# Writing a bias table to memory once, end first, instead of 129 times

## The chip, the core and the metric

The kernel runs on one core of one Trainium2 chip. A core has five engines that run side by side and wait for one another by semaphores: TensorE (PE, matrix products), VectorE (DVE), ScalarE (ACT), GpSimd (POOL) and SyncE (SP). 16 DMA engines move data between the device memory and the core's on-chip memory. The kernel starts its DMAs from three queues: SyncE's (q1 in the profile), ScalarE's (q10) and GpSimd's (q0). The metric is the device time of one execution in microseconds (us).

## The reference, cut to what matters

The program is three transformer blocks in a row over 256 tokens of width 1024. The change concerns only the first mixer, an attention with a selection of keys and a learned bias by the distance of key and query:

```
def t5_bucket(rel):            # 32 buckets of the distance key - query
    ...

def dsa_attention(q, k, v, iq, ik, iw, rel_bias):
    top_k = min(TOPK_MAX, seq // 4)                      # 64
    def block(i):
        s = einsum('bqhd,bsd->bqhs', iq_b, ik32) * idx_scale
        score = einsum('bqhs,bqh->bqs', relu(s), iw_b * w_scale)
        score = where(allowed, score, -inf)
        _, sel = lax.top_k(score, top_k)
        bias = rel_bias[t5_bucket(sel - t[None, :, None])]
        logits = einsum('bqhd,bqkhd->bhqk', q_b, k_sel) * att_scale + transpose(bias)
        p = softmax(where(valid, logits, -inf))
        return einsum('bhqk,bqkhd->bqhd', p, v_sel)
```

For each of 8 heads the bias depends on key minus query alone, so 384 numbers a head (distances -255 to 128) hold all that a block of 128 queries needs. Query row p wants a run of 256 of them whose start moves by one from row to row.

## The kernel before

The work goes through three mixers and two feed-forward blocks, then 16 experts. All weights are float32 and are split into a rounded part (`wh`, a cast on ScalarE, line 176) and a remainder (`wl`, a subtraction on VectorE or GpSimd, line 177) before TensorE uses them. This is done in *units* of 128x1024 numbers; a block of weights of 1 MB holds two units. Loads of blocks go out from SyncE into 5 buffers (`rawp`, line 67), so a load waits until the units of the block five loads before it are split. `take` (line 203) splits units three ahead of the one that TensorE is to use; there are 4 buffers each for `wh` and `wl`.

In the first mixer SyncE, ScalarE and GpSimd execute in the order in which the program issues; VectorE's and TensorE's order is fixed at build time. `ORDER_A` (line 1980) is the order of the program's steps. Those named below are:

- `iq0` to `iq7`, `aq0` to `aq3`, `ak0`, ...: one unit each of the projections, 24 matmuls of 256 columns (lines 237 to 239). Two units share a PSUM bank. For `iq`, each bank is emptied by two casts on ScalarE (line 740) and two subtractions on VectorE (line 741); only two banks exist (`psM`), so `iq6` cannot start before the bank of `iq2` and `iq3` is empty.
- `scb0` to `scb3`, `sca0`, `sca1`: selection scores (lines 747 to 766): matmuls, a Relu on ScalarE (757), multiply-adds on VectorE (763).
- `parms`: GpSimd issues 16 small loads of parameters (line 90). The last one, `gT`, is used by a multiplication on VectorE (`rw`, line 579) that stands in VectorE's order in front of the scores of `scb1`.
- `bias`: SyncE loads the bias rows (line 671) into `bias`, in the trace `b<-scr`.
- `selb0` to `selb7`, `sela0` to `sela7`: 8 rounds each of picking the 8 largest scores (lines 772, 773). In the last round the bias is added to the mask (line 779), half of the heads on VectorE and half on GpSimd: 128x1024 numbers each for the later 128 queries (`b<-b,score`), 128x512 for the first 128 (`ws<-b,score`).
- `lgb`, `lga`: logits, which take these sums (line 803).

The bias table comes about early: a one-hot matrix from `constants` (line 49) times `rel_bias` gives 8 rows of 384 numbers, ScalarE copies them from PSUM (line 664), and its queue then writes them to a scratch tensor in device memory 129 times for each head (lines 665, 666): 8 x 129 x 384 x 4 bytes = 1.585 MB. The load in line 671 steps by 383 numbers from one partition to the next, so that row p begins p numbers earlier in copy p of the table; that is what the copies are for.

Of the kernel before, what the change touches and what calls it, by code (L numbers as in the profile page):

```python
# [8 lines left out]
F32 = mybir.dt.float32  # L9
# [9 lines left out]
S = 256  # L19
# [9 lines left out]
def constants():  # L29

    p = np.arange(128)[:, None]
    f = np.arange(128)[None, :]
    eye = (p == f).astype(np.float32)
    upper = (p <= f).astype(np.float32)
    lower = (p >= f).astype(np.float32)
    base = np.concatenate([eye, upper, lower], axis=1).astype(np.float32)
    lev = []
    for b in (2, 4, 8, 16, 32, 64, 128):
        m = (p // b == f // b) & (p % b < b // 2) & (f % b >= b // 2)
        lev.append(m)  # L40
    lev = lev + [m.T for m in lev] + [p == f]
    levels = np.concatenate(lev, axis=1).astype(np.float32)
    rel = np.arange(384) - 255
    n = np.abs(rel)
    big = np.full(n.shape, 7)
    for edge in (8, 12, 16, 23, 32, 46, 64, 91):
        big = big + (n >= edge)
    bucket = np.where(rel > 0, 16, 0) + np.where(n < 8, n, big)
    onehot = (np.arange(32)[:, None] == bucket[None, :]).astype(np.float32)
    t = np.arange(S)  # L50
    inv = []
    for w in (2, 4, 8, 16):
        cnt = np.minimum(t + w - w // 2, S) - np.maximum(t - w // 2, 0)
        inv.append((np.float32(1.0) / cnt.astype(np.float32))[[*range(8), *range(S - 8, S)]])
    rows = np.concatenate([np.concatenate(inv), (t % 64 != 0).astype(np.float32), np.arange(CAP) + 1.0]).astype(np.float32)[None, :]
    return {"c_base": base, "c_levels": levels, "c_onehot": onehot, "c_rows": rows}


class Kernel:
# [569 lines left out]
    def mixer_ab(self):  # L629
        nc, I, sm = self.nc, self.I, self.sm  # L630
        with ExitStack() as st:
# [6 lines left out]
            onehot = sp.tile([32, 384], F32, name="onehot")  # L638
# [16 lines left out]
            p = self.mm()  # L655
# [6 lines left out]
            wsT = sp.tile([128, 8, 128], F32, name="wsT")  # L662
            bs = wsT[:8].rearrange("p a b -> p (a b)")[:, :384]
            nc.scalar.copy(bs, bt[:8, :384])
            scr = self.dram.tile([8, 129, 384], F32, name="scr")
            nc.scalar.dma_start(scr, bs[:, None, :].to_broadcast([8, 129, 384]))
            bias = b8()
            sc = scr[:, :, :]

            def bias_rows():  # L670
                self.load(bias, bass.AP(tensor=sc.tensor, offset=sc.offset + 127, ap=[[383, 128], [129 * 384, 8], [1, S]]))

            self.in_order("SP", "Activation", "Pool")
            kiw = sp.tile([80, S], F32, name="kiw")
# [70 lines left out]
            bp = {}  # L745

            def scores(t, h0, per):
# [17 lines left out]
                if h0 + 2 * per == 16:  # L765
                    nc.vector.memset(score[t][0:64, W - 64:W], NEG)

            def select(t, rounds):
                W = 128 * (t + 1)
                for i in rounds:  # L770
                    m8 = sm.tile([128, 8], F32, name="m8")
                    nc.vector.max(m8, score[t])
                    nc.vector.match_replace(score[t], m8, score[t], GONE)
                if rounds[-1] == 7:
                    nc.vector.tensor_scalar(score[t], score[t], GONE, NEG, op0=OP.not_equal, op1=OP.mult)
                    bp[t] = b8() if t else sp.tile([128, 8, 128], F32, name="ws")
                    for q in range(2):
                        a = slice(4 * q, 4 * q + 4)
                        self.on(f"bp{'ab'[t]}{q}").tensor_tensor(bp[t][:, a, :], bias[:, a, S - W:],
                                                                 score[t][:, None, :].to_broadcast([128, 4, W]), op=OP.add)  # L780

            qT = sp.tile([128, 4, S], F32, name="qT")
# [104 lines left out]
            def gated():  # L887
                for g in range(8):
# [5 lines left out]
            held, turns = [], []  # L894
            out = self.out_steps({0: ya, 4: yb}, ((0, 0), (1, 0), (0, 4), (1, 4)))
            steps = {"bias": bias_rows, "key0": index_keys, "key1": index_keys_turned, "parms": lambda: turns.extend(self.params(sp)),
                     "gvd": lambda: gv_done(held[0]), "gud": lambda: gu_done(held[1]), "gated": gated, "gate": gate,
                     "again": lambda: setattr(self, "g", self.gains())}
# [9 lines left out]
            for t, a in enumerate("ab"):  # L908
                steps.update((f"sel{a}{i}", lambda t=t, i=i: select(t, (i,))) for i in range(8))
                for q in range(2):  # L910
                    steps[f"ex{a}{q}"] = lambda t=t, q=q: expo(t, range(4 * q, 4 * q + 4))
                    steps[f"sh{a}{q}"] = lambda t=t, q=q: share(t, q)
                    steps[f"tu{a}{q}"] = lambda t=t, q=q: turn(t, q)
# [1171 lines left out]
```

## Time and profile before

| What | Before |
|---|---|
| median of 3 runs | 1848.58 us (1847.56 to 1848.87) |
| the profiled execution | 1848.39 us |
| its span in the trace | 1846.6 us |
| PE, DVE, ACT, POOL busy | 80%, 37%, 28%, 17% of the span |
| moved by q1, q10, q0 | 534.54, 1.59, 1.75 MB |

The page also cuts the span into 40 slices of 46 us and shows the busy share of each in tenths:

```profile
PE   7779999998899999889997566666566565656675
DVE  3675877758877777697410000000000000000001
...
DMA  8533654644335557322999999999999999999998
```

In the first three slices TensorE is less busy than in those after them. From slice 20 on the DMA engines are busy nearly all the time: the experts' weights. Between the two lies a long stretch in which TensorE is busy for 90% or more of most slices. [...]

### The profile page before, as it was taken

What the parts mean: (1) busy time and instruction counts of PE and PEld (TensorE: products, weight loads), DVE (VectorE), ACT (ScalarE), POOL (GpSimd) and SP (SyncE); (2) the same over time, 40 slices, a digit from 0 to 9 for tenths busy, and PEclk for the clock granted to TensorE, in tenths of its full rate; (3) what the DMA queues carried; (4) which work ended last, traced back from release to release, by engine and by line L of the source; (5) the groups of instructions that cost most, each with busy time, mean ns of one, the idle gap of its engine ahead of it and who ended that gap; (6) DMA issues with size and microseconds to landing.
All of it is one profiled execution on the core that took longest, in us unless ns stands there. A gap on an engine that the chain in (4) does not pass through costs nothing.

```text
span 1846.6 us, 22659 instructions
## 1 busy us (share of the span) xinstructions
PE 1468.6 (80%) x9340; PEld 923.8 (50%) x9340; DVE 692.1 (37%) x1143; ACT 518.0 (28%) x902; POOL 321.8 (17%) x339
## 2 busy tenths in 40 slices
PE   7779999998899999889997566666566565656675
PEld 6767999987779999778741111111111111111111
DVE  3675877758877777697410000000000000000001
ACT  4445655564446555553310000000000000000001
POOL 5453120044640001674200000000000000000000
PEclk9889999999999999899998778778877778887878
DMA  8533654644335557322999999999999999999998
GB/s 236 173 136 114 208 191 167 224 128 138 114 99 182 179 167 232 119 87 82 383 382 424 425 425 426 423 426 426 424 426 425 425 424 424 425 425 425 424 426 293
DMA packets 140665, 539.32 MB, mean 292 GB/s; under 512 B 6871, under 2 KB 85033, under 8 KB 109330
## 3 DMA queue, kind: packets, MB, share of 16 engines
q1 hardware_dynamic: 138434, 534.54, 73.8%
q10 hardware_dynamic: 1040, 1.59, 0.7%
q0 software_dynamic: 1088, 1.75, 0.4%
q8 instruction: 73, 1.20, 0.3%
q14 instruction: 30, 0.25, 0.0%
HBM read 535.21 MB, written 2.63 MB: 291 GB/s over the span
## 4 chain that ended last, share of the span: by engine, by line
DMA 47%; PE 37%; DVE 7%; issue 1%; ACT 1%; POOL 1%; POOLq 0%; DVEq 0%; SPq 0%; ACTq 0%
DMA w<-in_expert_w_up_dram 25%; DMA w<-in_expert_w_gate_dram 12%; DMA w<-in_expert_w_down_dram 10%; PE mm L237 3%; PE mm L238 3%; PE mm L239 3%; PE tp L237 2%; PE tp L238 2%; PE tp L239 2%; PE acc L956 2%; PE acc L958 2%; PE acc L957 2%; PE acc L249 2%; PE acc L250 2%; PE acc L251 2%
## 5 line engine op out<-in xcount | busy, mean ns | idle before, releaser
L1876 PE MATMUL mm<-w 128*32 128x512 f32 x1536 | 252.1, 752 | 157.7 <-DMA w<-in_expert_w_up_dram 101.6
L177 DVE TENSOR_TENSOR wl<-w,wh 128x1024 fp32r<-128x1024 f32 x180 | 248.1, 1381 | 66.0 <-ACT wh L176 65.5
L176 ACT CAST wh<-w 128x1024 fp32r<-128x1024 f32 x238 | 247.2, 1044 | 82.1 <-PE acc L958 35.9
L1896 PE MATMUL mm<-w,gain 128*32 128x512 f32 x512 | 165.8, 793 | 95.0 <-DMA w<-in_expert_w_down_dram 84.7
L1876 PEld LDWEIGHTS mm<-w 128*32 128x32 f32 x1536 | 50.7, 126 | 351.5 <-DMA w<-in_expert_w_up_dram 151.9
L1888 DVE TENSOR_TENSOR gain<-gain,mm 128x512 f32<-128x512 f32 x16 | 11.0, 688 | 561.3 <-PE mm L1876 561.3
L237 PE MATMUL mm<-xTh,wh 128*128 128x256 f32 x712 | 207.1, 291 | 12.6 <-DVE b L741 5.8
L238 PE MATMUL mm<-xTl,wh 128*128 128x256 f32 x712 | 205.3, 288 | 0.0
L239 PE MATMUL mm<-xTh,wl 128*128 128x256 f32 x712 | 205.0, 288 | 0.0
L1896 PE MATMUL tp<-w,gain 128*32 128x512 f32 (+1 forms) x544 | 165.6, 757 | 0.3 <-DMA w<-in_expert_w_down_dram 0.3
L177 POOL TENSOR_TENSOR wl<-w,wh 128x1024 fp32r<-128x1024 f32 x58 | 143.5, 2481 | 106.9 <-ACT wh L176 95.0
L1946 POOL TENSOR_SCALAR ss<-ss,ss 128x1 f32<-128x1 f32 x2 | 0.8, 410 | 922.9 <-ACT acc L1944 922.8
L237 PEld LDWEIGHTS mm<-xTh,wh 128*128 128x128 f32 x712 | 139.7, 196 | 16.1 <-issue 10.2
L238 PEld LDWEIGHTS mm<-xTl,wh 128*128 128x128 f32 x712 | 139.8, 196 | 2.3
L239 PEld LDWEIGHTS mm<-xTh,wl 128*128 128x128 f32 x712 | 139.5, 196 | 0.2
L1896 PEld LDWEIGHTS mm<-w,gain 128*32 128x32 f32 x512 | 28.4, 131 | 148.0 <-DMA w<-in_expert_w_down_dram 126.0
L237 PE MATMUL tp<-xTh,wh 128*128 128x256 f32 x352 | 99.6, 283 | 0.0
L238 PE MATMUL tp<-xTl,wh 128*128 128x256 f32 x352 | 99.6, 283 | 0.0
L239 PE MATMUL tp<-xTh,wl 128*128 128x256 f32 x352 | 99.5, 283 | 0.0
L1900 ACT COPY yv<-tp 128x512 f32<-128x512 f32 (+1 forms) x17 | 9.5, 560 | 307.5 <-PE acc L1903 306.0
L1876 PE MATMUL mm<-w,xg 128*32 128x512 f32 x512 | 75.4, 695 | 24.5 <-DMA w<-in_expert_w_up_dram 16.6
L1890 ACT COPY gain<-tp 128x512 f32<-128x512 f32 x16 | 9.4, 585 | 288.9 <-PE tp L277 288.9
(521 smaller groups left out, 2472.0 us busy)
## 6 DMA issues: line engine op xcount, KB each, us to landing
w<-in_expert_w_gate_dram SPq DMA_DIRECT2D x45, 2048.0 KB, 29.5
w<-in_expert_w_up_dram SPq DMA_DIRECT2D x45, 2048.0 KB, 29.6
w<-in_expert_w_down_dram SPq DMA_DIRECT2D x42, 2048.0 KB, 29.5
w<-in_ffn_w_up_dram SPq DMA_DIRECT2D x44, 1024.0 KB, 5.4
w<-in_expert_w_down_dram SPq DMA_DIRECT2D x40, 1024.0 KB, 29.5
w<-in_expert_w_gate_dram SPq DMA_DIRECT2D x38, 1024.0 KB, 29.5
w<-in_expert_w_up_dram SPq DMA_DIRECT2D x38, 1024.0 KB, 29.5
w<-in_ffn_w_down_dram SPq DMA_DIRECT2D x22, 1024.0 KB, 7.3
```

What stands on the lines that cost most here:

```text
L176: nc.scalar.copy(hv, v)
L177: (on[0] if on else self.low).tensor_tensor(lv, v, hv.bitcast(F32), op=OP.subtract)
L237: mm(ps, wh[:, k, :], xh[:, k, :], start=k == 0, stop=False)
L238: mm(ps, wh[:, k, :], xl[:, k, :], start=False, stop=False)
L239: mm(ps, wl[:, k, :], xh[:, k, :], start=False, stop=k == 7)
L249: self.nc.tensor.matmul(ps[t], a, wh[:, u, :], start=first and u == 0, stop=False)
L250: self.nc.tensor.matmul(ps[t], a, wl[:, u, :], start=False, stop=False)
L251: self.nc.tensor.matmul(ps[t], b, wh[:, u, :], start=False, stop=last and u == 1)
L956: nc.tensor.matmul(o, a, wh[:, c, :], start=False, stop=False)
L957: nc.tensor.matmul(o, a, wl[:, c, :], start=False, stop=False)
L1876: nc.tensor.matmul(p[32 * cb:32 * cb + 32, :], x(k), v[:, cb * 512:(cb + 1) * 512], start=k == 0, stop=k == 7)
L1896: nc.tensor.matmul(columns(py, c0, c1)[32 * row:32 * row + 32], h, v, start=start, stop=stop)
```

## The change

Three edits go together. The one-hot matrix is reversed, so each head's 384 numbers stand end first. The scratch tensor holds them once, 8 x 384 numbers (12 KB), and the load steps by one number from partition to partition, so that partition p reads numbers p + 1 to p + 256 of the reversed row. In `bias` the keys now run backwards; the two sums read them from the end, by an access pattern with a step of -1 (`turned`), on the same engines and with as many numbers as before.

```
-    onehot = (np.arange(32)[:, None] == bucket[None, :]).astype(np.float32)
+    onehot = (np.arange(32)[:, None] == bucket[None, ::-1]).astype(np.float32)
...
-            scr = self.dram.tile([8, 129, 384], F32, name="scr")
-            nc.scalar.dma_start(scr, bs[:, None, :].to_broadcast([8, 129, 384]))
+            scr = self.dram.tile([8, 384], F32, name="scr")
+            nc.scalar.dma_start(scr, bs)
             bias = b8()
-            sc = scr[:, :, :]
+            sc = scr[:, :]
...
-                self.load(bias, bass.AP(tensor=sc.tensor, offset=sc.offset + 127, ap=[[383, 128], [129 * 384, 8], [1, S]]))
+                self.load(bias, bass.AP(tensor=sc.tensor, offset=sc.offset + 1, ap=[[1, 128], [384, 8], [1, S]]))
...
+            def turned(v):
+
+                (p, q), (h, n), (c, w) = v.ap
+                return bass.AP(tensor=v.tensor, offset=v.offset + c * (w - 1), ap=[[p, q], [h, n], [-c, w]])
...
-                        self.on(f"bp{'ab'[t]}{q}").tensor_tensor(bp[t][:, a, :], bias[:, a, S - W:],
+                        self.on(f"bp{'ab'[t]}{q}").tensor_tensor(bp[t][:, a, :], turned(bias[:, a, :W]),
```

Every engine keeps its instructions in the same order; behind the new function the line numbers are higher by 5. The one instruction that changes its place or shape in a queue is the write, on ScalarE's queue near the program's start (`wsT` holds the 8 rows, `scr` is the scratch tensor, `wh` a rounded unit of weights):

```order
 L664 COPY wsT<-mm 8x384
 L675 COPY kiw<-mm 80x256
-L666 DMA scr<-wsT 1032x1x384
+L666 DMA scr<-wsT 8x384
 L176 CAST wh<-w 128x1024 x2
 L689 ACTIVATE dup,ssk<-tik 128x64 x2
```

The write stays between the same two instructions and covers 8 rows of 384 numbers instead of 1032.

## Rows read from the trace of the kernel before

**Rows 1.** The page: the chain that ended last, shares by engine:
```profile
DMA 47%; PE 37%; DVE 7%; issue 1%; ACT 1%; POOL 1%; POOLq 0%; DVEq 0%; SPq 0%; ACTq 0%
```

**Rows 2.** The write's DMA queue, 28 to 34 us: packets, MB, share of 16 engines:
```profile
q10 hardware_dynamic: 196, 0.30, 42.0%
```

**Rows 3.** The write's DMA queue from 50 to 53 us:
```profile
q10 hardware_dynamic: 66, 0.09, 23.2%
```

**Rows 4.** The SP DMA queue from the start to 28 us:
```profile
q1 hardware_dynamic: 6682, 7.21, 78.9%
```

**Rows 5.** Stretch; busy PE, PEld, DVE, ACT, POOL; PEclk; DMA share; GB/s:
```profile
16.00:18.00 2.00, 2.00 (x15) 1.82 (x14) 1.22 (x1) 2.00 (x4) 0.57 (x2) 1.00 1.09 347
32.00:34.00 2.00, 2.00 (x19) 2.00 (x18) 0.93 (x1) 0.00 (x0) 0.00 (x0) 1.00 0.52 86
40.00:42.00 2.00, 0.00 (x0) 0.00 (x0) 0.68 (x1) 1.23 (x3) 1.31 (x1) 0.71 0.51 81
44.00:46.00 2.00, 2.00 (x11) 2.00 (x11) 0.42 (x1) 0.01 (x1) 2.00 (x1) 0.50 0.92 221
```

**Rows 6.** DMA issues on SyncE, 24 to 28 us: start, us, engine, line:
```profile
25.16 9.20 SPq L87 DMA_DIRECT2D w<-in_ab_w_in_dram  x1
```

**Rows 7.** ScalarE in order of time, 16 to 60 us:
```profile
17.88 1.26 ACTq L666 DMA_DIRECT2D scr<-wsT  x1
...
30.62 1.05 ACT L176 CAST wh<-w 128x1024 fp32r<-128x1024 f32 x1
39.57 1.04 ACT L176 CAST wh<-w 128x1024 fp32r<-128x1024 f32 x1 [7.90 <-DMA w<-in_ab_w_in_dram]
40.64 0.58 ACT L740 CAST b<-mm 64x512 fp32r<-64x512 f32 x1
...
52.98 1.04 ACT L176 CAST wh<-w 128x1024 fp32r<-128x1024 f32 x1 [8.96 <-DMA w<-in_ab_w_in_dram]
...
56.93 1.08 ACT L757 ACTIVATE rl<-tp 128x512 f32<-128x512 f32 x2
57.90 1.05 ACT L176 CAST wh<-w 128x1024 fp32r<-128x1024 f32 x1
```

**Rows 8.** TensorE in order of time, 36 to 62 us:
```profile
37.26 0.28 PE L238 MATMUL mm<-xTl,wh 128*128 128x256 f32 x1
37.38 0.28 PE L239 MATMUL mm<-xTh,wl 128*128 128x256 f32 x1
43.42 0.55 PE L237 MATMUL mm<-xTh,wh 128*128 128x256 f32 x1 [5.76 <-DVE b L741]
```

**Rows 9.** GpSimd in order of time, 59 to 140 us:
```profile
59.02 2.37 POOL L177 TENSOR_TENSOR wl<-w,wh 128x1024 fp32r<-128x1024 f32 x1 [2.58 <-ACT wh L176]
61.33 0.81 POOL L90 DMA_DIRECT2D yb<-in_ffn_conv_w_dram  x1
...
72.97 0.75 POOL L90 DMA_DIRECT2D gT<-in_norm_ffn_w_dram  x1
...
109.06 2.38 POOL L779 TENSOR_TENSOR b<-b,score 128x1024 f32<-128x1024 f32 x1 [9.23 <-DVE score L775]
...
117.49 1.26 POOL L779 TENSOR_TENSOR ws<-b,score 128x512 f32<-128x512 f32 x1 [2.73 <-DVE score L775]
```

**Rows 10.** VectorE in order of time, 57 to 135 us:
```profile
76.48 0.42 DVE L579 TENSOR_TENSOR rw<-rw,gT 128x256 f32<-128x256 f32 x1 [5.94 <-DMA gT<-in_norm_ffn_w_dram]
...
109.50 3.03 DVE L779 TENSOR_TENSOR b<-b,score 128x1024 f32<-128x1024 f32 x1
...
117.52 1.78 DVE L779 TENSOR_TENSOR ws<-b,score 128x512 f32<-128x512 f32 x1
```

**Rows 11.** Busy time from 76.5 to 120 us, columns as in rows 5:
```profile
76.50:120.00 43.50, 30.54 (x181) 26.76 (x180) 41.59 (x86) 14.15 (x17) 20.33 (x9) 0.87 0.35 119
```

**Rows 12.** DMA issues: size in KB, median us from issue to landing:
```profile
b<-scr SPq DMA_DIRECT2D x1, 1024.0 KB, 10.3
...
gain<-in_mix_norm_dram SPq DMA_DIRECT2D x1, 512.0 KB, 8.4
```

## The prediction

> **What bounds the kernel now.** The page first: the chain that ended last is DMA for 47% and TensorE for 37% [rows 1]. The DMA part is the experts' stream at the end, TensorE's the stretch before it; both start when the work ahead of them is done, so time saved in the first mixer reaches the end, unless something there is late anyway. So I went to the mixer and asked of its first 120 us what ends each wait.
>
> The DMA queues by stretch come next. From 28 to 34 us q10, on which there is only the scratch write, holds 42.0% of the 16 engines' time (6.7 engines) and moves 0.30 MB, that is 50 GB/s [rows 2]. All queues together move 86 GB/s, and half of the engines are idle, the DMA share being 0.52; before the write, at 16 to 18 us, it was 347 GB/s at full share [rows 5]. The write goes out at 17.88 us [rows 7] and still holds 23.2% between 50 and 53 us [rows 3], that is to about 51.7 (23.2/42.0 of 3 us). It takes some 33 us, and a weight load, which has a part on every engine, ends only when its parts on those engines do: SyncE's issue at 25.16 us is held for 9.20 us [rows 6].
>
> The order of time on ScalarE shows the price: two casts wait 7.90 and 8.96 us for weights [rows 7]. ScalarE works in order, so behind the first the emptying of the PSUM bank stands still (L740, at 40.64), and TensorE, done with `iq5` at about 37.5, starts `iq6` at 43.42 [rows 8]. [...]
>
> Last, what follows. GpSimd starts the remainder of `aq2` at 59.02 and after it the parameter loads, from 61.33 to `gT` at 72.97 [rows 9]. VectorE waits 5.94 us for `gT` and goes on at 76.48 [rows 10]. From there to 120 us it is busy for 41.59 of 43.50 us [rows 11], so VectorE is the bound then, and its start is set by GpSimd's parameter loads, these by the remainder of `aq2`, and that by the weights.
>
> **The write goes.** Of 1032 rows 8 remain, under 1% of its DMA time. Are the weights then in time? By 28 us q1 had moved 7.21 MB [rows 4]. Issued until then are x (1.05 MB), three loads of 0.13, 0.07 and 0.52 MB, and seven blocks of 1.05 (the last at 25.16), 9.1 MB in all. 1.9 MB are open, 5.5 us at the 347 GB/s of 16 to 18 us [rows 5], so all would be there by 33.5, the block of `iq6` first, at about 28 to 30.
>
> The new timeline, with the durations of before:
> - ScalarE's cast of `iq5` ends at 30.62 + 1.05 = 31.7; that of `iq6` follows to 32.7 instead of starting at 39.57 [rows 7]. Its remainder on GpSimd takes 2.37 [rows 9]: 35.1.
> - The bank of `iq2` and `iq3`: from its first cast to TensorE's start were 2.8 us (40.64 to 43.42) [rows 7, 8]; now 32.7 + 2.8 = 35.5. TensorE ends `iq5` at 37.38 + 0.12 = 37.5 and finds both ready: its wait is gone.
> - `iq6` is 24 matmuls at 0.12 us (37.26 to 37.38) [rows 8], 2.9; the 8 of `scb0` take 1.0: 41.4. Two Relus, 1.08 [rows 7], to 42.5, and the cast of `aq2`. From its start to GpSimd's were 1.12 us (57.90 to 59.02) [rows 7, 9]: 43.6 instead of 59.02, 15.4 us earlier. The block of `aq2` (the load issued at 25.16) is there since 33.5.
> - `gT` follows as before: 76.48 - 59.02 = 17.46 us later [rows 9, 10], at 61.1. VectorE waits for it as before: its work ahead of `rw` took 76.48 - 5.94 - 59.02 = 11.5 us from the start of that remainder, so ends at 55.1.
> - From there on VectorE runs its 43.5 us, only 15.4 earlier. What is late next is `gT` still, not the weights.
>
> The sum holds two waits of 16.9 us, less what ScalarE would then wait for TensorE. [...]
>
> **The table is read from 12 KB.** The load still has 1024 rows of 1 KB. It took 10.3 us of landing; the nearest row for reading one place into all partitions is a gain row, 512 KB in 8.4 us, which makes 16.8 for 1 MB [rows 12]. It is used by the sums at 109 us [rows 10], which would be 94, and goes out at about 42, so I take 0. At the upper end its 6.5 us more fall on the parameter loads that share the engines with it, and so on `gT`. Less traffic beside them could bring `gT` up to 2 us earlier (an estimate: SyncE's loads, held back until about 58, are spread out from 33 on).
>
> **The sums read backwards.** No row has a step of -1. On GpSimd they take 2.38 and 1.26, on VectorE 3.03 and 1.78 [rows 9, 10]. VectorE's begin with GpSimd's and end 1.1 and 0.5 us after them (112.53 against 111.44, 119.30 against 118.75): VectorE seems to wait GpSimd's out and then run its own. So GpSimd's time stands on VectorE's path, 3.64 us in all, and VectorE's own 1.6. GpSimd's 2.38 for 1024 numbers is what its forward subtraction takes (2.37), so I take 0. [...]
>
> [...]
>
> **Sum.** 1848.39 (the profiled execution: span 1846.6 and 1.8 around it) - 15.4 = 1833.0. The median of the runs is 0.2 higher, so 1833.0 stands.
>
> **Rivals.**
> 1. *The reads from one place are slow.* The load of the table ties up the engines as the write did, and the parameter loads pay: 15.4 - 6.5, so 1839.5. For it: the 8.4 us of the gain row. Against it: that load shared the engines with weights.
> 2. *Reading backwards doubles the sums*: 1833.0 + 5.2 = 1838.2. Nothing in the trace speaks for or against it.
> 3. *Slower: GpSimd takes the step of -1 element by element.* Its 3.64 us stand on VectorE's path. It eats the gain at 15.4 / 3.64 = 4.2 times as much again, 5.2 times in all. At 7 times it adds 21.8, so 1854.8. Against it: the sums of before read the mask again for each head (a step of 0) and take no longer than the plain subtraction.
> 4. *The write is cheap and something else holds the weights.* At 347 GB/s 1.585 MB are 4.6 us, so 1843.8. If VectorE's chain is late anyway, nothing, 1848.4. Against it: q10's steady 42% and 50 GB/s.
>
> [...]
>
> **How the numbers follow.** Forecast 73%, its own range 1830.5 to 1836 (`gT` up to 2 us earlier; half of a doubled sum). Rival 1: 8%, rival 2: 10%, rival 3: 4%, rival 4: 5%. To leave out no more than 2 in 10 the range goes from 1829.5 to 1840.5 and so holds rivals 1 and 2. No change means within 0.2% (3.7 us), about what a measurement of this kernel can tell. Faster: forecast, rivals 1, 2 and part of 4, 0.93. Same: the rest of 4, and a part of 3, 0.04. Slower: 0.03.
>
> **What would show it.** In the new profile q10 carries some 0.01 MB; the DMA share of 0.5 at 28 to 52 us is gone; SyncE's issues take under 1 us; the two waits of 7.90 and 8.96 are under 1; TensorE runs through from 12 to about 50 us at full clock; GpSimd starts the parameter loads near 46 and `rw` runs near 61; the sums take 2.4 and 1.3 on GpSimd and are followed on VectorE as before; all later stages stand 15 us earlier. The prediction is wrong if `rw` does not move by 14 to 18 us, if the stretch of 43.5 us after it grows by more than 3, or if a weight load is still late after 30 us.

## The result, and the profile after

| | before | after |
|---|---|---|
| median of 4 runs | 1848.07 us (1847.37 to 1848.87) | 1833.53 us (1831.91 to 1835.29) |
| span of the profiled execution | 1846.6 us | 1832.8 us |

The ratio is 0.9924, with a 95% interval of 0.9912 to 0.9936: faster by 14.5 us, where 15.4 were forecast (1833.0 us, range 1829.5 to 1840.5).

The write is gone from the queues. First q10 on the page of the kernel after, for the whole span: packets, MB, share of 16 engines.

```profile
q10 hardware_dynamic: 16, 0.01, 0.0%
```

Then the DMA queues of the kernel after from 28 to 34 us; q10, which held 42.0% there [rows 2], has no row left.

```profile
q1 hardware_dynamic: 1060, 1.06, 54.9%
```

And the same from the start to 28 us:

```profile
q1 hardware_dynamic: 7516, 8.05, 88.0%
```

8.05 and 1.06 are 9.11 MB, all that the prediction counted (9.1), and it has landed by about 33 us: in the windows of the kernel after (columns as in [rows 5]) the DMA share from 32 to 34 us is 0.02. Before, 1.9 MB of it were open at 28 us, and from 28 to 34 q1 moved only 0.27 MB, though half of the engines were idle:

```profile
q1 hardware_dynamic: 266, 0.27, 12.9%
```

The windows of the kernel after, where PEclk is the granted clock of TensorE as a share of the full one:

```profile
32.00:34.00 2.00, 2.00 (x19) 2.00 (x18) 0.97 (x3) 1.89 (x3) 0.00 (x0) 1.00 0.02 7
40.00:42.00 2.00, 2.00 (x19) 2.00 (x18) 0.57 (x1) 0.58 (x1) 2.00 (x2) 1.00 0.28 59
44.00:46.00 2.00, 2.00 (x20) 2.00 (x19) 1.87 (x3) 1.59 (x3) 0.00 (x0) 1.00 0.27 103
63.50:107.00 43.50, 30.82 (x182) 26.86 (x181) 41.59 (x86) 14.10 (x17) 20.51 (x9) 0.90 0.35 121
```

TensorE works at full clock (1.00) at 40 and at 44 us, where before it was idle, with a granted clock of 0.71, and then worked at 0.50 [rows 5]. The last row is the 43.5 us from `rw` on: VectorE is busy for 41.59 us, to the hundredth as in [rows 11]. The stretch has only moved.

That a weight load has a part on every engine is seen where one block of weights moves alone, in the kernel after: 337 GB/s for 3 us, 1.01 of its 1.05 MB, at a DMA share of 0.98.

```profile
41.50:44.50 3.00, 3.00 (x27) 3.00 (x27) 1.97 (x3) 1.73 (x3) 1.19 (x1) 1.00 0.98 337
```

SyncE's issue of the block that was held for 9.20 us [rows 6], in the DMA issues of SyncE after, 24 to 30 us:

```profile
27.02 0.37 SPq L87 DMA_DIRECT2D w<-in_ab_w_in_dram  x1
```

ScalarE after, in order of time from 20 to 50 us (L is the line; the brackets at a row's end give the time for which the engine sat idle before it, and what released it). The two casts for `iq5` and `iq6` stand together at 32.69, and no row from 16 to 62 us waits for a DMA; the last row is the cast of `aq2` (57.90 in [rows 7]).

```profile
20.42 0.37 ACT L675 COPY kiw<-mm 80x256 f32<-80x256 f32 x1 [2.40 <-PE mm L233]
...
32.69 2.00 ACT L176 CAST wh<-w 128x1024 fp32r<-128x1024 f32 x2
...
45.38 1.05 ACT L176 CAST wh<-w 128x1024 fp32r<-128x1024 f32 x1
```

GpSimd after, 46 to 110 us: the remainder of `aq2`, the first and the last parameter load, the two sums (line 784 is 779 of before).

```profile
46.51 2.40 POOL L177 TENSOR_TENSOR wl<-w,wh 128x1024 fp32r<-128x1024 f32 x1 [3.81 <-ACT wh L176]
48.84 0.81 POOL L90 DMA_DIRECT2D yb<-in_ffn_conv_w_dram  x1
...
59.74 0.75 POOL L90 DMA_DIRECT2D gT<-in_norm_ffn_w_dram  x1
...
95.89 2.37 POOL L784 TENSOR_TENSOR b<-b,score 128x1024 f32<-128x1024 f32 x1 [9.23 <-DVE score L780]
...
104.32 1.27 POOL L784 TENSOR_TENSOR ws<-b,score 128x512 f32<-128x512 f32 x1 [2.73 <-DVE score L780]
```

VectorE after, same stretch:

```profile
63.50 0.42 DVE L579 TENSOR_TENSOR rw<-rw,gT 128x256 f32<-128x256 f32 x1 [5.96 <-DMA gT<-in_norm_ffn_w_dram]
...
96.32 3.02 DVE L784 TENSOR_TENSOR b<-b,score 128x1024 f32<-128x1024 f32 x1
...
104.34 1.79 DVE L784 TENSOR_TENSOR ws<-b,score 128x512 f32<-128x512 f32 x1
```

`rw` is 13.0 us earlier than in [rows 10] and still waits 6 us for `gT`. The sums are 13.2 us earlier and take what they took in [rows 9, 10]. The gain is still there later on: the last product of the third mixer (line 1438, now 1443) ends at 832.3 instead of 846.4, 14.1 us earlier, and the span is 13.8 shorter. The load of the table lands sooner than in [rows 12], by the issues of the kernel after:

```profile
b<-scr SPq DMA_DIRECT2D x1, 1024.0 KB, 7.3
```

### The profile page after: what moved, and what is told of

It reads as the page before. It is cut to its first block, busy times and chain, and to the rows that moved or that the text cites. A ratio compares the mean times of both kernels' runs of the same rounds, so it can differ in the third digit from the quotient of the medians.

```text
span 1832.8 us, 22659 instructions
## 1 busy us (share of the span) xinstructions
PE 1450.1 (79%) x9340; PEld 915.7 (50%) x9340; DVE 694.1 (38%) x1143; ACT 518.0 (28%) x902; POOL 322.9 (18%) x339
## 3 DMA queue, kind: packets, MB, share of 16 engines
HBM read 535.21 MB, written 1.06 MB: 293 GB/s over the span
## 4 chain that ended last, share of the span: by engine, by line
DMA 47%; PE 37%; DVE 7%; issue 1%; ACT 1%; POOL 1%; POOLq 0%; DVEq 0%; SPq 0%; ACTq 0%
DMA w<-in_expert_w_up_dram 25%; DMA w<-in_expert_w_gate_dram 12%; DMA w<-in_expert_w_down_dram 10%; PE mm L237 3%; PE mm L238 3%; PE mm L239 3%; PE tp L237 2%; PE tp L238 2%; PE tp L239 2%; PE acc L961 2%; PE acc L963 2%; PE acc L962 2%; PE acc L249 2%; PE acc L250 2%; PE acc L251 2%
## 5 line engine op out<-in xcount | busy, mean ns | idle before, releaser
L1881 PE MATMUL mm<-w 128*32 128x512 f32 x1536 | 255.8, 762 | 165.3 <-DMA w<-in_expert_w_up_dram 100.6
L1901 PE MATMUL mm<-w,gain 128*32 128x512 f32 x512 | 157.8, 763 | 102.1 <-DMA w<-in_expert_w_down_dram 91.9
L1901 PE MATMUL tp<-w,gain 128*32 128x512 f32 (+1 forms) x544 | 157.6, 728 | 0.8 <-DMA w<-in_expert_w_down_dram 0.8
```

The lines of the kernel that those rows point to most:

```text
L1881: nc.tensor.matmul(p[32 * cb:32 * cb + 32, :], x(k), v[:, cb * 512:(cb + 1) * 512], start=k == 0, stop=k == 7)
L1901: nc.tensor.matmul(columns(py, c0, c1)[32 * row:32 * row + 32], h, v, start=start, stop=stop)
```

## Experiments

The theory was the prediction's: the long write delays weight blocks, and the rest of the change costs and gives nothing. Its rivals were that part of the gain is the reading of a small table or lost to the backward sums, that the write costs by its bytes, and that it costs in proportion to its length and not by due times. All ratios are to the kernel before, on the same chip.

### Is it the write, and only the write?

**All copies written again.** The changed kernel, with 129 copies written and copy 0 read.

```
-            scr = self.dram.tile([8, 384], F32, name="scr")
-            nc.scalar.dma_start(scr, bs)
+            scr = self.dram.tile([8, 129, 384], F32, name="scr")
+            nc.scalar.dma_start(scr, bs[:, None, :].to_broadcast([8, 129, 384]))
...
-                ... ap=[[1, 128], [384, 8], [1, S]]))
+                ... ap=[[1, 128], [129 * 384, 8], [1, S]]))
```

> The changed kernel with the 129 copies written again; the load still reads one copy of each head (step 1 from partition to partition) and the sums still read backwards. If the write is what cost the time: 1848 (1845 to 1850), the write's queue at some 42% of the DMA engines' time from 28 to 34 us, two waits of ScalarE for weights of 7 to 9 us, and VectorE at the multiplication rw near 76 us. Rival, the gain came from the load's shorter span or from its reading out of 12 KB: 1833 to 1836 and rw near 63 us, since the load is as in the changed kernel.

Measured: 1847.69 us, ratio 0.9999 (0.999 to 1.0007). The queues from 28 to 34 us, ScalarE's waits and `rw` on VectorE are those of before:

```profile
q10 hardware_dynamic: 199, 0.31, 41.7%
q1 hardware_dynamic: 227, 0.23, 10.8%
```

ScalarE of the same run, from 16 to 62 us, the two long waits:

```profile
39.30 1.04 ACT L176 CAST wh<-w 128x1024 fp32r<-128x1024 f32 x1 [8.05 <-DMA w<-in_ab_w_in_dram]
...
52.31 1.04 ACT L176 CAST wh<-w 128x1024 fp32r<-128x1024 f32 x1 [8.56 <-DMA w<-in_ab_w_in_dram]
```

VectorE of the same run:

```profile
75.66 0.42 DVE L579 TENSOR_TENSOR rw<-rw,gT 128x256 f32<-128x256 f32 x1 [5.78 <-DMA gT<-in_norm_ffn_w_dram]
```

This kernel reads backwards and reads only one copy of each head, and is as slow as before: the whole gain is the write, and the other two edits sum to nothing, within 2 us.

**Sums read forwards.** The changed kernel without the step of -1; the keys get the biases in reversed order, so its output is another.

```
-                        ... tensor_tensor(bp[t][:, a, :], turned(bias[:, a, :W]),
+                        ... tensor_tensor(bp[t][:, a, :], bias[:, a, :W],
```

> The changed kernel, but the sums read the keys forwards (the biases then belong to the wrong keys, so this leaves out the turning). If a step of -1 costs nothing: 1833.5 within 1.5, the sums 2.37 and 1.27 us on GpSimd, 3.02 and 1.79 on VectorE as with the turned read. Rival, the backward read has a price that the lock between the two engines hides: the GpSimd sums are shorter than 2.3 and 1.2 and the kernel is 1 to 4 us faster, 1829.5 to 1832.5.

Measured: 1834.5 us, ratio 0.9926 (0.9911 to 0.9941), the same as with the step of -1. GpSimd of this run from 42 to 110 us:

```profile
43.00 2.39 POOL L177 TENSOR_TENSOR wl<-w,wh 128x1024 fp32r<-128x1024 f32 x1 [2.93 <-ACT wh L176]
...
92.40 2.38 POOL L784 TENSOR_TENSOR b<-b,score 128x1024 f32<-128x1024 f32 x1 [9.22 <-DVE score L780]
...
100.86 1.26 POOL L784 TENSOR_TENSOR ws<-b,score 128x512 f32<-128x512 f32 x1 [2.73 <-DVE score L780]
```

2.38 and 1.26 us forwards, 2.37 and 1.27 backwards: the step costs nothing there, and nothing on VectorE, where it takes 3.02 and 1.79 backwards and, forwards, 3.03 and 1.78, in this run as in [rows 10]:

```profile
92.84 3.03 DVE L784 TENSOR_TENSOR b<-b,score 128x1024 f32<-128x1024 f32 x1
...
100.88 1.78 DVE L784 TENSOR_TENSOR ws<-b,score 128x512 f32<-128x512 f32 x1
```

What the expectation calls the lock between the two engines was measured in the kernel before as follows. VectorE's subtraction of 128x1024 numbers takes 1.22 us at 78.33, where GpSimd is idle, and 3.13 at 112.71 beside one of GpSimd's, and ends 1.08 us after it:

```profile
78.33 1.22 DVE L177 TENSOR_TENSOR wl<-w,wh 128x1024 fp32r<-128x1024 f32 x1
...
112.71 3.13 DVE L177 TENSOR_TENSOR wl<-w,wh 128x1024 fp32r<-128x1024 f32 x1
```

```profile
111.40 3.36 POOL L177 TENSOR_TENSOR wl<-w,wh 128x1024 fp32r<-128x1024 f32 x1
```

A second thing is to be seen. The remainder of `aq2` starts at 43.00 us, 3.5 us before that of the changed kernel, though the two kernels are alike up to there. On VectorE:

```profile
59.82 0.42 DVE L579 TENSOR_TENSOR rw<-rw,gT 128x256 f32<-128x256 f32 x1 [5.79 <-DMA gT<-in_norm_ffn_w_dram]
```

**The changed kernel once more**, unedited, to see how much its start varies.

> The changed kernel once more, for its start and its spread. In its first profile the copy of the index keys (line 675) ran at 20.42 us, 2.7 us later than before, and rw at 63.50. If that start was chance: the copy at 17 to 18 us this time, rw near 60 to 61 as forecast, and times again spread between 1831 and 1836. Rival, the change delays the start: the copy at 20 us again.

Measured: 1836.37 us (1832.59 to 1840.66), ratio 0.9941 (0.9927 to 0.9954). On ScalarE `kiw`, near the write, starts at 19.43 us here, at 20.42 in the first profile of the changed kernel, and at 17.66 in the run with forward sums and 17.76 in that of before. So neither the 17 to 18 nor the 20 us that were expected came; but the change is not what delays the start, since the run with forward sums, which is the same program up to there, starts as before did. In the ten profiles in which the table is made as here (all but those from 128 and 16 partitions, below) `kiw` starts between 17.32 and 20.56 us.

The traces show where the time goes. In the late profiles TensorE runs its first products slowly: the two of line 661 take 1.44 us in the first profile of the changed kernel

```profile
14.99 1.44 PE L661 MATMUL mm<-onehot,relb 32*8 32x384 f32 x2
```

and 0.81 in that of before:

```profile
13.69 0.81 PE L661 MATMUL mm<-onehot,relb 32*8 32x384 f32 x2
```

From 12 to 16 us TensorE runs 24 matmuls in the profile of before and 24 with forward sums, but 10 in the first profile of the changed kernel, 15 in its repeat and 14 in the first run of SyncE's loads (below), in all three of which `kiw` comes after 18 us. The granted clock is not what sets these three apart: from 12 to 16 us it is 0.81 and 0.79 in the first two and 1.00 in the three late ones. In the first profile of the changed kernel VectorE too takes 2 us longer, for the two instructions of line 377 (2.97 us instead of 0.88). Why an execution begins one way or the other was not tested.

Two distances from `kiw` measure the mixer without its start. The remainder of `aq2` comes 26.1 us after it in both profiles of the changed kernel (46.51 - 20.42 and 45.51 - 19.43) and 25.3 with forward sums; the forecast was 25.8 (43.6 - 17.76), before it was 41.3. `rw` comes 44.3 us after it here (63.77 - 19.43), 43.1 in the first profile and 42.2 with forward sums; the forecast was 43.3 (61.1 - 17.76), before it was 58.7. The second distance also holds the landing of `gT`, which takes 2.9 to 5.1 us from the start of its issue to `rw` over the profiles in which GpSimd issues it, so the first is the sharper measure.

### What makes the write long, and when does it cost?

**The same table from 128 partitions.** The kernel before; the products are made so that each of 128 partitions holds one head's 384 numbers, and each is written 8 times (1024 rows instead of 1032).

```
-            nc.tensor.matmul(bt[:8, :384], relb, onehot, start=True, stop=True)
+            rel16 = ...; nc.vector.tensor_copy(rel16, relb[:, :, None].to_broadcast([32, 8, 16]))
+            nc.tensor.matmul(bt[:, :384], rel16..., onehot, start=True, stop=True)
...
-            nc.scalar.dma_start(scr, bs[:, None, :].to_broadcast([8, 129, 384]))
+            nc.scalar.dma_start(scr, bs[:, None, :].to_broadcast([128, 8, 384]))
```

> The kernel before with nearly the same bytes (128 copies instead of 129, 1.57 MB), written from 128 partitions that hold each head's row 16 times, 8 copies from each, instead of from 8 partitions. If the write is slow because it runs on 7 or 8 of the 16 engines, at some 0.2 us a row on each: 1024 rows on 16 engines take 12 to 15 us, the write ends near 34 us, its queue's share goes well above 42%, ScalarE's long waits shrink to under 4 us, and the time is 1833 to 1840. Rival, the memory takes the write no faster whichever engines carry it (50 GB/s): it lasts until 50 us or more, now on all engines, and the time is 1847 to 1856.

Measured: 1836.15 us, ratio 0.9941 (0.9927 to 0.9955). The queues from 30 to 32 us:

```profile
q10 hardware_dynamic: 326, 0.49, 65.0%
q1 hardware_dynamic: 298, 0.29, 41.7%
```

The write, issued at 21.20 us, is over at about 32.3 (from 32 to 34 it has 3.8%), in 11 us from its issue instead of 34 (17.88 to 51.7 before), and weights move beside it. A row of 1.5 KB takes 64 ns of an engine here (0.65 x 16 x 2 us / 326) and 206 before (0.42 x 16 x 6 / 196). From 20 to 62 us no cast waits for weights. Yet `rw` comes 48.8 us after `kiw`, not 43 to 44: the added copy on VectorE makes TensorE late near the start, which is the cost of this experiment's own set-up, not of the write. TensorE waits for the copy, and ScalarE's activation of line 689 starts 10.5 us after `kiw` (27.49 - 17.01), where it is 6.2 in the changed kernel (26.60 - 20.42). So the 4 us are lost by then, and the only cast in between that waits for weights does so for 1.02 us at 18.38, before the write is issued:

```profile
19.75 0.91 PE L661 MATMUL mm<-onehot,rl 32*128 32x384 f32 x2 [2.59 <-DVE rl L661]
```

```profile
27.49 0.26 ACT L689 ACTIVATE dup<-tik 128x64 f32<-128x64 f32 x1 [2.46 <-DVE tik L687]
```

**The same from 16 partitions**, 64 times each, with the same set-up (`[16, 64, 384]`):

```
+            nc.scalar.dma_start(scr, bs[:, None, :].to_broadcast([16, 64, 384]))
```

> The kernel before with 1024 rows written from 16 partitions that hold each head's row twice, 64 copies from each, so that all 16 engines take part as from 128 partitions, but each reads one partition again and again, as in the kernel before. From 128 partitions a row cost some 64 ns of an engine, from 8 partitions 206. If the number of engines alone made the write slow: as from 128 partitions, its queue near 65% with 300 rows in 2 us, done by 33 us, 1834 to 1838. If reading the same partition again and again makes the row dear: some 0.2 us a row on each engine, 64 rows on each, so 13 us or more at full share, done near 36 us or later beside the weights, and 1837 to 1843.

Measured: 1837.82 us, ratio 0.9949 (0.9935 to 0.9962). The queues from 30 to 32 us:

```profile
q10 hardware_dynamic: 129, 0.20, 81.4%
q1 hardware_dynamic: 122, 0.12, 17.1%
```

Nearly all engines work at the write now, twice as many as before, but a row still takes 202 ns of one (0.814 x 16 x 2 / 129). So the number of engines alone does not make the write slow: with 8 source partitions about half of the engines were busy, with 16 nearly all, and a row cost three times as much in both as with 128. Two readings are left, and these runs do not separate them. Either there are two causes that multiply, the engines that take part and a row that is dear because one partition is read 64 or 129 times; or there is one, a limit on what a source partition gives. For the second speaks that the rate goes with the partitions: 50 GB/s from 8 (0.30 MB in 6 us), 100 from 16 (0.20 MB in 2 us), 6.3 GB/s for each in both, while 128 gave 245 in all (0.49 MB in 2 us), 1.9 for each. The write ends at about 39 us; no cast waits for weights after 20 us, and `rw` comes 48.7 us after `kiw`, as from 128 partitions. The time lies in the range that was expected for dear rows, but also in that for the engines alone; it is the cost of a row, 202 ns, that decides.

**32, 64 and 96 copies written for nothing.** The changed kernel with a second write of n copies to a tensor that nobody reads, right behind the first:

```
+            junk = self.dram.tile([8, n, 384], F32, name="junk")
+            nc.scalar.dma_start(junk, bs[:, None, :].to_broadcast([8, n, 384]))
```

> The changed kernel plus a write of 32 copies of the table (256 rows) to a scratch tensor that nobody reads, from the same 8 partitions, on the same queue. If the cost is a due time: at 8 rows in some 0.25 us the write ends near 27 us, before ScalarE wants the block of iq6 at 31.7, and the time stays at 1833.5 within 1.5. Rival, the cost goes with the rows: 256/1032 of the 14.5 us, so 1837.

> The same with 64 copies (512 rows). Due time: the write ends near 35 us, the block of iq6 lands 2 to 4 us late and the one of aq0 hardly, 1835 to 1838. Rival, the cost goes with the rows: half of the 14.5 us, 1840.7.

> The changed kernel plus a write of 96 copies that nobody reads. 32 and 64 copies cost the first mixer nothing that can be seen (VectorE at rw 44.3 and 43.0 us after the copy of the index keys, against 43.1 and 44.4 without). If the cost is a due time: the write ends near 44 us, past the due times of the blocks of iq6 (32 to 35) and aq0 (36 to 38), VectorE is at rw 47 to 54 us after that copy, and the time 1838 to 1845. Rival, what costs is not this write at all but the load that waits for it, or the copies in the memory: rw as with 64 copies, 1833 to 1837.

| copies | median us | ratio (95%) | write over, us | longest wait for weights on ScalarE after 25 us | remainder of `aq2` after `kiw`, us | `rw` after `kiw`, us |
|---|---|---|---|---|---|---|
| 0 (second set of runs) | 1836.37 | 0.9941 (0.9927 to 0.9954) | - | none | 26.1 | 44.3 |
| 32 | 1835.54 | 0.9935 (0.9923 to 0.9948) | 28 | none | 25.8 | 44.3 |
| 64 | 1836.19 | 0.994 (0.9927 to 0.9952) | 38 | 1.40 | 26.1 | 43.0 |
| 96 | 1841.65 | 0.9971 (0.9961 to 0.9982) | 46.5 | 3.97 | 30.2 | 47.5 |
| 129 (all copies written again) | 1847.69 | 0.9999 (0.999 to 1.0007) | 51 | 8.56 | 41.0 | 58.3 |

The waits of 1.40 and 3.97, on ScalarE with 64 copies

```profile
39.49 1.05 ACT L176 CAST wh<-w 128x1024 fp32r<-128x1024 f32 x1 [1.40 <-DMA w<-in_ab_w_in_dram]
```

and with 96:

```profile
49.59 1.05 ACT L176 CAST wh<-w 128x1024 fp32r<-128x1024 f32 x1 [3.97 <-DMA w<-in_ab_w_in_dram]
```

Half of the copies cost nothing that can be measured, though the write goes on to 38 us; with 64 copies, from 30 to 32 us:

```profile
q10 hardware_dynamic: 64, 0.10, 42.4%
```

From 64 to 96 copies 5 us are added, from 96 to 129 another 6 by the medians. In the profiles the second step is 7.6 us at `rw` (68.04 against 75.66) and 10.8 counted from `kiw`. The profile with 96 copies is one that starts late: its extra write was issued at 21.15 us instead of 17.46, and q1 had moved 8.57 MB by 34 us instead of 7.48. So the size of that step mixes the copies with the start. A cost in proportion, 15.4 x 64 / 129 = 7.6 us, is excluded by the run with 64 copies. Nobody reads these copies, so it is the write that costs and not a load that waits for it.

The blocks that came late are not those that were expected. With 64 copies that of `iq6` is in time, and that of `aq0` is 1.40 us late, which costs nothing further on (26.1 in the table); with 96 both are in time, and that of `aq2` is 3.97 late. The median with 32 copies, 1835.54, is above the 1832 to 1835 expected, but not above that of the changed kernel in the same set of runs. The main reading holds: the write costs only where it is still going when a block is due.

### Can the next wait go too?

**The router's rows and `gT` on SyncE's queue.** In the changed kernel `rw` waits for `gT`, the last of GpSimd's loads. Here both come by SyncE, ahead of that list.

```
-        self.param(self.gT.rearrange(...
+        self.load(self.gT.rearrange(...
```

(The same for `rw`, whose buffer is cleared near the start.)

> The changed kernel with the last three parameter loads (the router's weights and gT) issued on SyncE's queue instead of at the end of GpSimd's, and rw cleared near the start. In the changed kernel VectorE still waits 5.96 us for gT. If that wait sets the pace of the first mixer as I said: it goes, VectorE goes on with the scores near 57.5 us, and the time falls by 3 to 6 us to 1827.5 to 1830.5 (some of it lost because TensorE has the scores of scb2 ready only near 60). Rival, the weights or TensorE are what is late there: no change, 1832 to 1835.

Measured: 1831.82 us, ratio 0.9915 (0.9902 to 0.9928). VectorE of this run, 38 to 62 us:

```profile
39.76 1.56 DVE L579 TENSOR_TENSOR rw<-rw,gT 128x256 f32<-128x256 f32 x1 [2.62 <-DMA gT<-in_norm_ffn_w_dram]
...
59.03 1.00 DVE L763 SCALAR_TENSOR_TENSOR score<-rl,tiw,score 128x256 f32<-128x256 f32 x2 [1.34 <-ACT rl L757]
```

`rw` runs at 39.76, and its wait of 5.96 us has become one of 2.62 at an earlier place. Now VectorE waits 1.34 us for the Relu (in the second run, below, the Relu in its turn waits up to 2.0 us for TensorE's scores), and the sums start at 91.51 us on GpSimd instead of 95.89, 4.4 us earlier. Of these 1.6 are the earlier start (`kiw` at 18.78 instead of 20.42): counted from `kiw` the sums start after 72.7 us, against 75.5 and 77.1 in the two profiles of the changed kernel and 74.7 with forward sums. The median is 1.7 and 4.6 us below the two of the changed kernel (1833.53 and 1836.37), and between what was expected, 1827.5 to 1830.5, and the rival's 1832 to 1835.

**The same again**, beside other runs:

> The kernel with the last three parameter loads on SyncE's queue once more, to settle whether it beats the changed kernel (1833.5 and 1836.4 in two sets of runs; this one 1831.8). If the stage's gain of some 4 us reaches the end: 1831 to 1833 again, every run below 1834.5. Rival, the last set was lucky in the last expert, where the changed kernel's times spread by 4 us: 1834 to 1837.

Measured: 1833.35 us (1828.93 to 1834.62), ratio 0.9918 (0.9903 to 0.9932). The median and the slowest run lie just above what was expected (1833, and every run below 1834.5). Both ratios are below the changed kernel's (0.9915 and 0.9918 against 0.9924 and 0.9941), but the intervals overlap. In the profiles the sums start 74.2 us after `kiw` here (91.67 - 17.46), half a us before those of the run with forward sums. Whether it beats the changed kernel stays open.

## Why the prediction was right

- *The write bounds the stretch from 28 to 52 us*: right, and shown twice, by putting it back (nothing gained) and by its copies in steps. That a late block is the way by which it costs is shown too: the waits for weights come and go with it (7.90 and 8.96 us before, none after, 8.05 and 8.56 with the copies back). Rival 4, a cheap write, fell with the first.
- *The weights are there by 33.5*: right, about 33. Issues held: 0.37 us instead of 9.20.
- *GpSimd 15.4 us earlier, at 43.6*: the term was sound, and the first profile does not show it (46.51), because its first 20 us ran 2.7 us late (`kiw` at 20.42 against 17.76). With forward sums and a punctual start it is 43.00, and counted from `kiw` it is 26.1 and 25.3 where 25.8 were forecast. I had taken the start of before as fixed, and TensorE as at full speed from 12 us on; in the first profile line 661 shows it slow at 15.
- *`gT` 17.46 later*: 16.99 in the changed kernel (63.50 - 46.51), 16.82 with forward sums, but 18.26 in the repeated profile (63.77 - 45.51). That is 0.6 us earlier to 0.8 later than forecast; the prediction allowed 2 us to the early side.
- *The sign that I had set*, `rw` 14 to 18 us earlier: by the letter it speaks against the prediction, with 13.0 us in the first profile and 12.7 in the repeated one. Counted from `kiw` it is 15.6 and 14.4, and 16.7 with forward sums as it stands. The sign did not allow for a start that moves.
- *VectorE's 43.5 us unchanged*: right.
- *The table from 12 KB costs 0*: right, 7.3 us instead of 10.3; rival 1 fell. *The backward sums cost 0*: right, 2.37 and 1.27 us on GpSimd against 2.38 and 1.26 forwards; rivals 2 and 3 fell. The 5.2 us of rival 2 were the 3.64 and 1.6 us of the sums taken once more, and no run shows such a doubling.
- *The sum*: 15.4 forecast; 14.5 by the first medians and 10.6 by the second (1847.01 - 1836.37). Both are inside the range; the second, 1836.37, is just outside the forecast's own 1830.5 to 1836. That the first came within half a us of 1833.0 is partly luck, since the medians of one kernel differ by 2.8 us.

What the prediction did not price is the scatter: a start that moves by 3 us, and the end, below.

## What to carry to other kernels

Look at a long DMA by the engines that it holds and by what is due on other queues while it lasts; here 1.6 MB from 8 partitions were harmless up to the first late block and cost 11 to 15 us beyond it. In the kernel before it showed as a DMA share of 0.52 at 32 us [rows 5], with waits for weights of 7.90 and 8.96 us beside it [rows 7]. Before counting a difference of 2 or 3 us as an effect, measure it against a point inside the kernel that the change cannot touch, as `kiw` here; without that, 1.6 of the 4.4 us in the last experiment would have passed for an effect.

## What was not expected

The end of the kernel has two forms. The stretch from 32 to 16 us before the end, in the windows of before, then of the changed kernel, then of its repeated run, with the 4 us behind it:

```profile
1814.60:1830.60 16.00, 13.99 (x62) 4.02 (x61) 1.38 (x2) 2.63 (x5) 0.00 (x0) 0.79 1.01 343
1830.60:1834.60 4.00, 3.46 (x36) 1.64 (x35) 2.67 (x4) 1.82 (x5) 0.00 (x0) 1.00 0.87 280
```

After:

```profile
1800.80:1816.80 16.00, 13.99 (x63) 4.25 (x62) 1.70 (x3) 2.63 (x5) 0.00 (x0) 0.79 1.02 344
```

After, repeated:

```profile
1806.90:1822.90 16.00, 14.00 (x57) 3.54 (x56) 1.38 (x2) 2.11 (x5) 0.00 (x0) 0.56 0.98 320
1822.90:1826.90 4.00, 3.46 (x35) 1.42 (x34) 2.67 (x4) 1.82 (x5) 0.00 (x0) 1.00 0.11 35
```

With a granted clock of 0.79 in the 16 us, weights still land in the 4 us behind them (DMA share 0.87); with 0.56 they have landed by then (0.11) and TensorE is still working through them (busy for 3.46 of the 4 us). From the third mixer's last product to the end it is 1000.2 us before and 1000.5 after, but 1003.9 in the repeated run, 1003.7 with forward sums and with the second run of SyncE's loads, and 1003.8 with the write from 128 partitions. In the other eight of the twelve profiles it is 999.8 to 1001.2. So the two forms are some 3.5 us apart, and the changed kernel shows both. What decides which form an execution takes was not tested. With the 3 us of the start it would make up most of the scatter within the changed kernel's runs (1831.9 to 1840.7); that they belong together is an inference, and no run tested it.
